# A hybrid delta-rule and mLSTM layer: gate rows in quarters on a ring of their own, scratch transfers later, and a first chunk made by hand

## The chip, the cores and the metric

The kernel runs on one core of one Trainium2 chip. The metric is the device time of one execution in microseconds (us), as the median of several runs. A core has five engines that take instructions in order, each from its own queue: TensorE (PE in the profile; matrix products and transposes), VectorE (DVE), ScalarE (ACT), GpSimd (POOL) and SyncE (SP), which here only issues DMA transfers. An instruction waits on semaphores for what it needs, and everything behind it on the same engine waits with it. On-chip memory is SBUF for operands and PSUM for results of products.

## The reference

One layer on x of 256 rows by 2048 columns, all float32. Of `reference.py`, cut to what matters here:

```python
shift, scale, gate = split(silu(c) @ w_ada + b_ada, 3)     # w_ada: 2048 x 6144
h = rms_norm(x, norm_pre_w) * (1 + scale) + shift
qkv, a, b, z, ml_qk, ml_v, ml_i, ml_f, ml_o, ml_z, g_A, g_B = split(h @ w_in)
# branch A: causal conv and silu on qkv, gated delta rule over 32 value heads in chunks of 64
#   (in each chunk a unit lower triangular system is solved), head norm, times silu(z)
y_A = o_a @ w_proj_gdn                                      # 4096 -> 2048
# branch B: conv and silu on ml_qk, chunkwise mLSTM over 8 heads, head norm, sigmoid(ml_o), silu(ml_z)
y_B = h_b @ w_proj_mlstm                                    # 2048 -> 2048
out = (sigmoid(g_A) * y_A + sigmoid(g_B) * y_B) @ w_out
return x + gate * rms_norm(out, norm_post_w)
```

## The kernel before, in words

Nearly all of the work is products of the 256 rows of h (later y and the merged rows) with weights that are read once. Each float32 operand is split into a high part that TensorE takes in one pass (`hi`, a cast on ACT, line 169) and the remainder (`lo`, a subtraction on VectorE or POOL, line 170), and each product is three: hi·hi, hi·lo, lo·hi (`mm3`, line 223).

**The stream.** `Stream` takes a list of units written out by hand. A weight unit is 1 MB: 128 partitions by 2048 columns, loaded by SP into `raw` of a ring of three buffers (`load_w`, line 164), prepared as two pieces of 1024 columns (`prep_w`: `whi`, `wlo`, four buffers each), and used piece by piece by TensorE. Preparation runs a few pieces ahead of use. A load is issued, in the order of the list, as soon as the unit that many places back on its ring has been prepared; a unit whose buffer isn't free holds every load behind it. During the start part POOL makes the remainder of some pieces in place of VectorE (`share`); the other pieces, and all later ones, are VectorE's.

**Side work.** After each used piece `side.step()` lets every open side generator run one step. All that isn't streaming, as the convolutions, decays, triangular inverses and norms, is written as generators whose `yield`s place their instructions between the pieces; `wait(n)` lets n steps pass, and `side.debt` and `side.room` hold back VectorE work where much of it stands in line. A piece takes TensorE about 2.7 to 3 us.

**The start.** `csil` is silu(c) spread over 128 partitions, made by eight products of one row (`one_row` by `crow`, line 282). For each chunk k of 128 of the 2048 columns of h, VectorE multiplies the two transposed rows of w_ada for shift and scale with `csil` and sums them (`ar` tiles, a ring of three of 1 MB, line 355). `x_scale` scales two chunks of x by the row norm on ACT (line 302), `x_turn` transposes them on TensorE and copies them back on ACT (lines 308 and 310). `h_chunk` makes shift and scale on ACT, then `hf` (ACT, line 333), `h_hi` (ACT), `h_lo` (VectorE or POOL). While these chunks come one by one, TensorE works on fourteen column groups of w_in that the branches don't need first (`START`, in seven `BLOCKS` of a range of k): partial sums over a few chunks are kept in `part` tiles (copies on ACT, line 413, additions on VectorE, line 411). The last two numbers of a block are the times, counted in w_ada rows, at which those rows are due in the list.

**The gdn periods.** Eight periods (`gdn_period`), each with three projections: q, k, v of a head pair, z, and q, k, v of the second pair. Behind the first and third follows `gdn_stage1`: convolution, decay rows `gb` read from DRAM (line 611), masks on POOL (line 618), exponentials on ACT (line 626), scores. `block_rows` writes the diagonal 32x32 blocks of the scores to DRAM (`ud`). `base_inverse` reads them back spread over partitions (`ug`), inverts them on VectorE, writes the result `xx` to DRAM (`xd`, line 745), reads it back in another order (`xcmp`, four transfers, line 748), copies it into `x0` on ACT (line 755) and transposes it into `ycmp` on VectorE (line 752). `gdn_stage2` uses both in small products (`mp`, line 781, to `po`). All of these transfers and the loads of the weights are issued by SP, in the order in which the steps reach them.

**mLSTM, gate and end.** Four mLSTM units follow. Among their weights stand sixteen units with the rows of w_ada for the gate (`add_gate_unit`), loaded on the ring of the weights; VectorE multiplies each by a value of `sil` and adds it to `gacc` in two halves of 1024 columns (line 1089). Then come the projections of y (`add_proj_y`, with `ya` read from DRAM and split into `yhi`, `ylo`), the merge and the output projection.

Of the kernel before, what the change touches and what calls it, by code (L numbers as in the profile page):

```python
# [117 lines left out]
def hybrid_layer_kernel(  # L118
# [51 lines left out]
        (eng or V).tensor_tensor(lo, src, hi.bitcast(F32), op=ALU.subtract)  # L170

    share = [-3072.0, START_SHARE]

    def split_w(src, hi, lo):

# [8 lines left out]
    def prep_w(h, raw, width=2048):  # L184
        n = min(1024, width - h * 1024)
        hi = wp.tile([P, 1024], F32R, name="whi", tag="whi", bufs=4)
        lo = wp.tile([P, 1024], F32R, name="wlo", tag="wlo", bufs=4)
        split_w(raw[:, h * 1024:h * 1024 + n], hi[:, 0:n], lo[:, 0:n])
        return hi, lo

# [35 lines left out]
    bp = x0 = y0 = None  # L226


    ct = const("ct", c_t, [P, KC])
    sil = cp.tile([P, KC], F32, name="sil")  # L230
    A.activation(sil, ct, AF.Silu)
# [36 lines left out]

    pcs = ExitStack()
    csil = pcs.enter_context(tc.tile_pool(name="pcs", bufs=1, space=PSUM)).tile([P, D], F32, name="csil")  # L270
    crow = [part[4 + i].rearrange("p b c -> p (b c)")[0:1] for i in range(2)]
    for i in range(2):
        SP.dma_start(crow[i], c_row[:, i * 1024:(i + 1) * 1024])
    for b in range(2):
        SP.dma_start(xs[:, b], x[b * P:(b + 1) * P])
    SP.dma_start(ident, consts[:, 0:128])
    bat = const("bat", b_ada_t, [P, 32])
    npre = const("npre", npre_t, [P, KC])
    for i in range(2):
        A.activation(crow[i], crow[i], AF.Silu)  # L280
    for q in range(4):
        T.matmul(csil[:, q * 512:(q + 1) * 512], one_row, crow[q // 2][:, (q % 2) * 512:(q % 2 + 1) * 512],
                 start=True, stop=True)
    late_c = {}

    def late_consts():
        SP.dma_start(con[:, 128:512], consts[:, 128:512])
        late_c.update(gcv=const("gcv", gconv, [P, 256]), mcv=const("mcv", mconv, [P, 64]),
                      abb=const("abb", ab_bias, [P, 1]), alog=const("alog", a_log, [32, 1]),
                      gnw=const("gnw", gnorm, [P, 1]), mnw=const("mnw", mnorm_t, [P, KC]))  # L290

    for b in range(2):
        A.activation(part[2].rearrange("p b c -> p (b c)"), xs[:, b, 0:1024], AF.Square, accum_out=ss[:, b, 0:1])
        V.scalar_tensor_tensor(part[3].rearrange("p b c -> p (b c)"), xs[:, b, 1024:D], 1.0, xs[:, b, 1024:D],
                               op0=ALU.mult, op1=ALU.mult, accum_out=ss[:, b, 1:2])
    V.tensor_reduce(rs, ss, axis=AX.X, op=ALU.add)
    V.tensor_scalar(rs, rs, 1.0 / D, EPS, op0=ALU.mult, op1=ALU.add)
    pow_(rs, rs, mhalf[:, 0:2])

    def x_scale(k):  # L300
        for b in range(2):
            A.activation(xs[:, b, k * P:(k + 2) * P], xs[:, b, k * P:(k + 2) * P], AF.Copy, scale=rs[:, b:b + 1])

    def x_turn(k):
        ps = jtile("xps")
        for b in range(2):
            for kk in range(2):
                T.transpose(ps[:, (b * 2 + kk) * P:(b * 2 + kk + 1) * P], xs[:, b, (k + kk) * P:(k + kk + 1) * P],
                            ident)
        A.copy(xs[:, :, k * P:(k + 2) * P], ps.rearrange("p (b c) -> p b c", b=2))  # L310
# [9 lines left out]
    V.scalar_tensor_tensor(bnp, bat[:, KC:2 * KC], 1.0, npre, op0=ALU.add, op1=ALU.mult)  # L320

    def load_ada(src):
        raw = sp.tile([P, 2048], F32, name="ar", tag="ar", bufs=ADA_BUFS)
        SP.dma_start(raw, src)
        return raw

    def h_chunk(k):

        A.activation(sh[:, k:k + 1], ad[:, k:k + 1], AF.Identity, bias=bat[:, k:k + 1])
        A.activation(s1[:, k:k + 1], ad[:, KC + k:KC + k + 1], AF.Identity, bias=bnp[:, k:k + 1],  # L330
                     scale=npre[:, k:k + 1])
        hf = sp.tile([P, S], F32, name="hf", tag="hf", bufs=2)
        A.activation(hf.rearrange("p (b t) -> p b t", b=2), xs[:, :, k * P:(k + 1) * P], AF.Identity, bias=sh[:, k:k + 1], scale=s1[:, k:k + 1])
# [6 lines left out]
    BLOCKS = ((EARLY, 0, 1, 1.1, 3.5), (REST, 0, 2, 4, 8), (EARLY, 1, 3, 8, 12), (REST, 2, 2, 12, 16.5),  # L340
              (ALL, 4, 4, 16.5, 26), (ALL, 8, 4, 26, 32), (ALL, 12, 4, 32, 32))
    due = []

# [5 lines left out]
    def ada_units():  # L349

        adders = []
        for k in range(KC):
            for pt in range(2):
                def prep(h, raw, k=k, pt=pt):
                    V.scalar_tensor_tensor(raw, raw, 1.0, csil, op0=ALU.mult, op1=ALU.mult,
                                           accum_out=ad[:, pt * KC + k:pt * KC + k + 1])
                    j = 2 * (2 * k + pt) - 4
                    if 4 <= j < 16:
                        x_turn(j)
                        if j < 12:  # L360
                            x_scale(j + 4)
                    h_chunks(k - 1)
                    if pt == 1:
                        due.append(k)
                        if k == 0:
                            h_chunks(0)
                        elif k == KC - 1:
# [27 lines left out]
    def add_start_groups(bi):  # L395
# [136 lines left out]
        stream.add(w_ab, prep_w, use, after=lambda: side.add(gates(st_["ps"])))  # L532

    ada = ada_units()
    ia = 0
    for bi, (groups, k0, nk, first, last) in enumerate(BLOCKS):
        if bi == len(BLOCKS) - 1:
            add_ab()
        fs = add_start_groups(bi)
        for j, f in enumerate(fs):  # L540
            ahead = first + (last - first) * j / len(fs)
            while ia < len(ada) and ia < ahead:
                ada[ia]()
                ia += 1
            f()

# [83 lines left out]
    def gdn_stage1(p, ps, res):  # L630
# [50 lines left out]
        for blk, ps_, n, c0 in ((0, psa, 256, 0), (1, psb, 128, 512)):  # L681
# [10 lines left out]
                pow_(sk, sse[:, 2:4], phalf[:, 0:2])  # L692
            else:
                scored[0] = p
        block_rows(res, z)
# [15 lines left out]

    def base_inverse(zg, res, zr):

        ud = res["ud"]
# [15 lines left out]
        for i in range(1, 32, 2):  # L730
# [10 lines left out]
            if w == 2:  # L741
                V.scalar_tensor_tensor(xx[:, 0:nq, i + 1], xx[:, 0:nq, i], nsu[:, i // 2:i // 2 + 1],
                                       xx[:, 0:nq, i + 1], op0=ALU.mult, op1=ALU.add)
        yield from wait(1)
        SP.dma_start(xd.rearrange("qq q rg m i -> (q rg m) qq i"), xx)
        xcmp = bp.tile([P, 8, 32], F32, name="xcmp", tag="xcmp", bufs=1)
        for q in range(4):
            SP.dma_start(xcmp[32 * q:32 * q + 32], xd[:, q])
# [3 lines left out]
        V.transpose(ycmp.rearrange("p m i -> p (m i)"), xcmp.rearrange("p m i -> p (m i)"))  # L752
# [317 lines left out]
    gate_at = [0, 0]  # L1070
    gate_half = []

    def add_gate_unit():

        gate_at[1] += KC
# [4 lines left out]
        gate_at[0] += 1  # L1080

        def prep(h, raw):
            side.debt += 2.4
            for q in range(2):
                if i == 0:
                    gate_half.append(bp.tile([P, 1024], F32, name=f"gacc{q}", tag=("ug", "rr")[q], bufs=1 + q))
                    V.tensor_scalar(gate_half[q], raw[:, q * 1024:(q + 1) * 1024], sil[:, 0:1], None, op0=ALU.mult)
                else:
                    V.scalar_tensor_tensor(gate_half[q], raw[:, q * 1024:(q + 1) * 1024], sil[:, i:i + 1],
                                           gate_half[q], op0=ALU.mult, op1=ALU.add)  # L1090
# [315 lines left out]
```

## Time and profile before

| | us |
|---|---|
| runs of the kernel before | 1602.19, 1605.75, 1607.46 (median 1605.75) |
| the profiled execution | 1603.88 |
| its span, first to last instruction | 1601.9 |
| TensorE busy | 1577.8 (98 %) |
| VectorE busy | 1150.1 (72 %) |
| ScalarE busy | 941.0 (59 %) |
| GpSimd busy | 236.7 (15 %) |

The span leaves out about 2 us of the execution. Times in rows are counted from the span's start. A timeline row gives the start, the duration, the engine, the line in the kernel, the operation, output and inputs with their shapes, how many such operations follow each other, and in brackets the idle time before them and what ended it; SPq is SP's queue of DMA issues. TensorE's matmuls overlap, so the duration of one is longer than the distance to the next. The mean granted clock of TensorE is 0.999.

### The profile page before, as it was taken

Reading aid. Unit: us, or ns where it says so; the run is one execution under the profiler, and the core shown is the slowest. Engines: PE = TensorE matmul, PEld = TensorE weight load, DVE = VectorE, ACT = ScalarE, POOL = GpSimd, SP = SyncE. Lnnn points to the kernel's source line nnn. Section 1 sums busy time; section 2 is a strip of 40 time slices with the busy share of each in tenths; the row PEclk is TensorE's granted clock in tenths of the full one; section 3 lists DMA queues with packets and bytes.
Section 4 is the critical chain, followed back from the end, with each engine's and each line's share of the span. In section 5 each row is a group of like instructions: output and inputs, shape, how many; then the busy total and the mean of one; then the engine's idle time right before and its main releaser. Section 6 shows DMA issues by size and latency. Waiting matters only on the chain.

```text
span 1601.9 us, 25461 instructions
## 1 busy us (share of the span) xinstructions
PE 1577.8 (98%) x9844; PEld 1388.1 (87%) x9844; DVE 1150.1 (72%) x1801; ACT 941.0 (59%) x1503; POOL 236.7 (15%) x193
## 2 busy tenths in 40 slices
PE   7999999999999999999999999999999999999998
PEld 4888888899999999999999999889988888888886
DVE  6695556765689788887888788776878556756654
ACT  7754446765656575757576666655565644444443
POOL 1787771000000010000000000000000000100100
PEclk9999999999999999999999999999999999999999
DMA  9898775965565646564656465566888667766573
GB/s 375 339 406 335 279 274 195 289 238 191 170 203 175 205 148 204 164 193 169 193 169 195 149 197 176 187 214 247 290 308 305 227 249 284 283 246 244 200 273 113
DMA packets 96261, 372.37 MB, mean 232 GB/s; under 512 B 26262, under 2 KB 46214, under 8 KB 58252
## 3 DMA queue, kind: packets, MB, share of 16 engines
q1 hardware_dynamic: 96140, 370.75, 66.2%
q8 instruction: 77, 1.26, 0.3%
q14 instruction: 44, 0.36, 0.1%
HBM read 354.40 MB, written 16.31 MB: 231 GB/s over the span
## 4 chain that ended last, share of the span: by engine, by line
PE 79%; issue 13%; DMA 3%; DVE 2%; ACT 2%; POOL 1%; SPq 0%; DVEq 0%; POOLq 0%; ACTq 0%
PE pn L223 35%; PE pt L223 28%; PE py L223 8%; DMA raw<-in_dram 1%; POOL mg L1196 1%; PE psa L223 1%; ACT whi L169 1%; DVE wlo L170 1%; DMA ya<-o_dr 1%; DMA ar<-in_dram 1%; PE mz L816 0%; PE mq L807 0%; PE pa L828 0%; PE po L856 0%; PE po L857 0%
## 5 line engine op out<-in xcount | busy, mean ns | idle before, releaser
L170 DVE TENSOR_TENSOR wlo<-raw,whi 128x1024 fp32r<-128x1024 f32 x454 | 561.5, 1245 | 253.9 <-ACT whi L169 248.8
L169 ACT CAST whi<-raw 128x1024 fp32r<-128x1024 f32 (+1 forms) x517 | 533.0, 1046 | 327.1 <-PE pn L223 148.1
L223 PE MATMUL pt<-h_hi,whi 128*128 128x256 f32 x1280 | 367.8, 287 | 0.0
L223 PE MATMUL pt<-h_hi,wlo 128*128 128x256 f32 x1280 | 362.0, 283 | 0.0
L223 PE MATMUL pt<-h_lo,whi 128*128 128x256 f32 x1280 | 362.0, 283 | 0.0
L223 PE MATMUL pn<-whi,h_hi 128*128 128x512 f32 x896 | 353.9, 395 | 6.6 <-ACT whi L169 5.7
L223 PE MATMUL pn<-wlo,h_hi 128*128 128x512 f32 x896 | 350.0, 391 | 1.1 <-POOL wlo L170 0.6
L223 PE MATMUL pn<-whi,h_lo 128*128 128x512 f32 x896 | 349.8, 390 | 0.0
L223 PEld LDWEIGHTS pt<-h_hi,whi 128*128 128x128 f32 x1280 | 245.3, 192 | 1.4
L223 PEld LDWEIGHTS pt<-h_lo,whi 128*128 128x128 f32 x1280 | 245.4, 192 | 0.3
L223 PEld LDWEIGHTS pt<-h_hi,wlo 128*128 128x128 f32 x1280 | 245.2, 192 | 0.0
L223 PEld LDWEIGHTS pn<-whi,h_hi 128*128 128x128 f32 x896 | 168.8, 188 | 42.5 <-ACT whi L169 6.1
L223 PEld LDWEIGHTS pn<-wlo,h_hi 128*128 128x128 f32 x896 | 168.8, 188 | 36.0 <-DVE wlo L170 1.3
L223 PEld LDWEIGHTS pn<-whi,h_lo 128*128 128x128 f32 x896 | 168.6, 188 | 35.3
L170 POOL TENSOR_TENSOR wlo<-raw,whi 128x1024 fp32r<-128x1024 f32 (+1 forms) x63 | 146.3, 2332 | 67.1 <-ACT whi L169 64.9
L223 PE MATMUL py<-whi,yhi 128*128 128x512 f32 x384 | 150.6, 392 | 0.7 <-ACT vt L1017 0.7
L223 PE MATMUL py<-whi,ylo 128*128 128x512 f32 x384 | 149.6, 390 | 0.0
L223 PE MATMUL py<-wlo,yhi 128*128 128x512 f32 x384 | 149.4, 389 | 0.0
L411 DVE TENSOR_TENSOR part<-pn,part 128x512 f32<-128x512 f32 x112 | 73.7, 685 | 52.6 <-PE pn L223 52.6
L169 ACT CAST yhi<-ya 128x512 fp32r<-128x512 f32 x48 | 29.9, 622 | 130.9 <-PE py L223 127.4
L170 DVE TENSOR_TENSOR ylo<-ya,yhi 128x512 fp32r<-128x512 f32 x48 | 33.2, 692 | 86.7 <-ACT yhi L169 78.7
L593 DVE SCALAR_TENSOR_TENSOR qs<-pt,gcv,qs 128x255 f32<-128x255 f32 (+2 forms) x192 | 92.2, 480 | 4.6
(251 smaller groups left out, 1790.8 us busy)
## 6 DMA issues: line engine op xcount, KB each, us to landing
raw<-in_dram SPq DMA_DIRECT2D x259, 1024.0 KB
ar<-in_dram SPq DMA_DIRECT2D x32, 1024.0 KB
raw<-in_dram SPq DMA_DIRECT2D x16, 512.0 KB
ya<-o_dr SPq DMA_DIRECT2D x32, 256.0 KB
gate_dr<-part SPq DMA_DIRECT2D x11, 512.0 KB
gb<-rows SPq DMA_DIRECT2D x20, 256.0 KB
raw<-in_dram SPq DMA_DIRECT2D x6, 768.0 KB
ug<-ud SPq DMA_DIRECT2D x32, 128.0 KB
```

What stands on the lines that cost most here:

```text
L169: A.copy(hi, src)
L170: (eng or V).tensor_tensor(lo, src, hi.bitcast(F32), op=ALU.subtract)
L223: T.matmul(ps, l, r, start=start and i == 0, stop=stop and i == 2, skip_group_check=True)
L411: V.tensor_tensor(part[g][:, b], ps[b], part[g][:, b], op=ALU.add)
L593: V.scalar_tensor_tensor(dst[:, n, sh:], src[:, 0:S - sh], taps(n, 3 - sh), dst[:, n, sh:], op0=ALU.mult, op1=ALU.add)
L1196: G.tensor_tensor(mcols(b, hf, cg), mcols(b, hf, cg), s_, op=ALU.add)
```

## The change

Four parts.

1. *The start.* `c_row` is issued from ACT's queue, `ar0` (the first shift row) ahead of x on SP, the first scale row `ar1` in two halves behind x; three small constants are issued from POOL's queue; `ct` and its silu move to the later constants. A function `first_chunk` takes the place of the preparation of the first weight piece: it puts five calls of a float32 product of zeros behind csil on TensorE, the squares of x's rows (three of four on ACT, one on VectorE), the norm's small steps on POOL, the two sums of chunk 0 on VectorE, the copy of the first `whi` on VectorE, x_scale(0), x_turn(0), another product of zeros, and makes `hf` straight from PSUM. x_turn(2), x_scale(4) and x_scale(6) move in between the first groups. The units of w_ada start at chunk 1; one pair of due times goes from 12 to 13.
2. *h_chunk.* `h_lo` of the last chunk is VectorE's.
3. *Scratch.* `block_rows` comes one step later; `base_inverse` begins with a step, and its wait for `ug` is one step shorter; `xd` is written one step later; `xcmp` is read two steps after that, and used two steps on in place of five.
4. *Gate rows.* Each unit is loaded as four quarters of 512 columns into buffers of `yhi` and `ylo`, on a ring "gate" of one, and summed in four quarters.

```diff
-    crow = [part[4 + i].rearrange("p b c -> p (b c)")[0:1] for i in range(2)]
-    for i in range(2):
-        SP.dma_start(crow[i], c_row[:, i * 1024:(i + 1) * 1024])
+    crow = ada_tile()[0:1]
+    A.dma_start(crow, c_row)
+    ar0, ar1 = load_ada(w_ada[0]), ada_tile()
     for b in range(2):
         SP.dma_start(xs[:, b], x[b * P:(b + 1) * P])
-    SP.dma_start(ident, consts[:, 0:128])
-    bat = const("bat", b_ada_t, [P, 32])
-    npre = const("npre", npre_t, [P, KC])
+    for t, src in ((bat, b_ada_t), (npre, npre_t), (ident, consts[:, 0:128])):
+        G.dma_start(t, src)
...
+    def keep_busy(n):
+
+        for _ in range(n):
+            T.matmul(zps, zero[:, 0:P], zero, start=True, stop=True)
...
-        A.copy(xs[:, :, k * P:(k + 2) * P], ps.rearrange("p (b c) -> p b c", b=2))
-    for k in range(0, 8, 2):
-        x_scale(k)
-        if k in (2, 4):
-            x_turn(k - 2)
+        if k:
+            A.copy(xs[:, :, k * P:(k + 2) * P], ps.rearrange("p (b c) -> p b c", b=2))
...
+    def first_chunk(src, hi, lo):
+        keep_busy(5)
...
+        ada_sum(ar0, slice(0, D), ad[:, 0:1])
+        V.scalar_tensor_tensor(bnp, bat[:, KC:2 * KC], 1.0, npre, op0=ALU.add, op1=ALU.mult)
+        for i in range(2):
+            ada_sum(ar1, half[i], adh[:, i:i + 1])
...
+        V.tensor_copy(hi, src)
+        x_scale(0)
+        xps = x_turn(0)
+        keep_busy(1)
+        V.tensor_tensor(lo, src, hi.bitcast(F32), op=ALU.subtract)
+        hf = sp.tile([P, S], F32, name="hf", tag="hf", bufs=2)
+        A.activation(hf.rearrange("p (b t) -> p b t", b=2), xps[:, :, 0], AF.Identity, bias=sh[:, 0:1],
+                     scale=s1[:, 0:1])
+        split(hf, h_hi[:, 0], h_lo[:, 0], V)
+        A.copy(xs[:, :, P:2 * P], xps[:, :, 1])
+        x_scale(2)
...
-        split(hf, h_hi[:, k], h_lo[:, k], V if k < 2 else G)
+        split(hf, h_hi[:, k], h_lo[:, k], V if k in (1, KC - 1) else G)
...
-    (EARLY, 1, 3, 8, 12), (REST, 2, 2, 12, 16.5),
+    (EARLY, 1, 3, 8, 13), (REST, 2, 2, 13, 16.5),
...
+                    if bi == 0 and gg == 3:
+                        x_turn(2)
+                    elif gg == (NE - 1, NE)[min(bi, 1)] and c == 0 and bi < 2:
+                        x_scale(4 + 2 * bi)
...
+        yield
         block_rows(res, z)
-        yield
...
     def base_inverse(zg, res, zr):
+        yield
...
-        yield from wait(4)
+        yield from wait(3)
...
-        yield from wait(1)
+        yield from wait(2)
         SP.dma_start(xd.rearrange("qq q rg m i -> (q rg m) qq i"), xx)
+        yield from wait(2)
...
-        yield from wait(5)
+        yield from wait(2)
...
+    def load_gate(src):
+        raw = [yp.tile([P, 512], F32, name=f"graw{q}", tag=("yhi", "ylo")[q % 2], bufs=2) for q in range(4)]
+        for q in range(4):
+            SP.dma_start(raw[q], src[:, q * 512:(q + 1) * 512])
+        return raw
...
-            side.debt += 2.4
-            for q in range(2):
+            side.debt += 2.6
+            for q in range(4):
...
-        stream.add(w_ada[32 + i], prep, None, 1)
+        stream.add(w_ada[32 + i], prep, None, 1, load=(load_gate, "gate", 1))
```

More of the change, by code (lines that the diff above doesn't have):

```diff
@@ L172, in hybrid_layer_kernel @@
     share = [-3072.0, START_SHARE]
+    begin = []
     def split_w(src, hi, lo):
@@ L187, in prep_w @@
         lo = wp.tile([P, 1024], F32R, name="wlo", tag="wlo", bufs=4)
+        if begin:
+            begin.pop()(raw[:, 0:n], hi, lo)
+            return hi, lo
         split_w(raw[:, h * 1024:h * 1024 + n], hi[:, 0:n], lo[:, 0:n])
@@ L270, in hybrid_layer_kernel, with ada_tile, load_ada, silu_c @@
     csil = pcs.enter_context(tc.tile_pool(name="pcs", bufs=1, space=PSUM)).tile([P, D], F32, name="csil")
-    crow = [part[4 + i].rearrange("p b c -> p (b c)")[0:1] for i in range(2)]
-    for i in range(2):
-        SP.dma_start(crow[i], c_row[:, i * 1024:(i + 1) * 1024])
+    def ada_tile():
+        return sp.tile([P, 2048], F32, name="ar", tag="ar", bufs=ADA_BUFS)
+    def load_ada(src):
+        raw = ada_tile()
+        SP.dma_start(raw, src)
+        return raw
+    crow = ada_tile()[0:1]
+    A.dma_start(crow, c_row)
+    ar0, ar1 = load_ada(w_ada[0]), ada_tile()
     for b in range(2):
         SP.dma_start(xs[:, b], x[b * P:(b + 1) * P])
-    SP.dma_start(ident, consts[:, 0:128])
-    bat = const("bat", b_ada_t, [P, 32])
-    npre = const("npre", npre_t, [P, KC])
+    bat = cp.tile([P, 32], F32, name="bat")
+    npre = cp.tile([P, KC], F32, name="npre")
+    for t, src in ((bat, b_ada_t), (npre, npre_t), (ident, consts[:, 0:128])):
+        G.dma_start(t, src)
     for i in range(2):
-        A.activation(crow[i], crow[i], AF.Silu)
+        SP.dma_start(ar1[:, i * 1024:(i + 1) * 1024], w_ada[1][:, i * 1024:(i + 1) * 1024])
+    for i in range(2):
+        A.activation(crow[:, i * 1024:(i + 1) * 1024], crow[:, i * 1024:(i + 1) * 1024], AF.Silu)
     for q in range(4):
-        T.matmul(csil[:, q * 512:(q + 1) * 512], one_row, crow[q // 2][:, (q % 2) * 512:(q % 2 + 1) * 512],
-                 start=True, stop=True)
+        T.matmul(csil[:, q * 512:(q + 1) * 512], one_row, crow[:, q * 512:(q + 1) * 512], start=True, stop=True)
+    zero = part[-1][:, 0]
+    G.memset(zero, 0.0)
+    zps = jtile("zps")
+    def keep_busy(n):
+        for _ in range(n):
+            T.matmul(zps, zero[:, 0:P], zero, start=True, stop=True)
     late_c = {}
+    def silu_c():
+        yield
+        yield
+        A.activation(sil, ct, AF.Silu)
     def late_consts():
         SP.dma_start(con[:, 128:512], consts[:, 128:512])
+        SP.dma_start(ct, c_t)
+        side.add(silu_c())
         late_c.update(gcv=const("gcv", gconv, [P, 256]), mcv=const("mcv", mconv, [P, 64]),
@@ new lines, in x_turn, with ada_sum @@
+        return ps.rearrange("p (b k t) -> p b k t", b=2, k=2)
+    bnp = sp.tile([P, KC], F32, name="bnp")
+    adh = sp.tile([P, 2], F32, name="adh")
+    def ada_sum(raw, cols, out):
+        V.scalar_tensor_tensor(raw[:, cols], raw[:, cols], 1.0, csil[:, cols], op0=ALU.mult, op1=ALU.mult,
+                               accum_out=out)
+    def first_chunk(src, hi, lo):
+        keep_busy(5)
+        half = [slice(i * 1024, (i + 1) * 1024) for i in range(2)]
+        for b in range(2):
+            for i in range(2):
+                if b == 0 and i == 1:
+                    V.scalar_tensor_tensor(part[3].rearrange("p b c -> p (b c)"), xs[:, b, half[i]], 1.0,
+                                           xs[:, b, half[i]], op0=ALU.mult, op1=ALU.mult, accum_out=ss[:, b, i:i + 1])
+                else:
+                    A.activation(part[2].rearrange("p b c -> p (b c)"), xs[:, b, half[i]], AF.Square,
+                                 accum_out=ss[:, b, i:i + 1])
+        G.tensor_tensor(rs, ss[:, :, 0], ss[:, :, 1], op=ALU.add)
+        G.tensor_scalar(rs, rs, 1.0 / D, EPS, op0=ALU.mult, op1=ALU.add)
+        pow_(rs, rs, mhalf[:, 0:2])
+        ada_sum(ar0, slice(0, D), ad[:, 0:1])
+        V.scalar_tensor_tensor(bnp, bat[:, KC:2 * KC], 1.0, npre, op0=ALU.add, op1=ALU.mult)
+        for i in range(2):
+            ada_sum(ar1, half[i], adh[:, i:i + 1])
+        V.tensor_tensor(ad[:, KC:KC + 1], adh[:, 0:1], adh[:, 1:2], op=ALU.add)
+        V.scalar_tensor_tensor(s1[:, 0:1], ad[:, KC:KC + 1], npre[:, 0:1], bnp[:, 0:1], op0=ALU.mult, op1=ALU.add)
+        A.activation(sh[:, 0:1], ad[:, 0:1], AF.Identity, bias=bat[:, 0:1])
+        V.tensor_copy(hi, src)
[9 more added lines that the diff above has]
+        x_scale(2)
@@ L327, in h_chunk @@
+    begin.append(first_chunk)
     def h_chunk(k):
@@ L351, in ada_units @@
         adders = []
-        for k in range(KC):
+        for k in range(1, KC):
             for pt in range(2):
@@ L541, in hybrid_layer_kernel @@
             ahead = first + (last - first) * j / len(fs)
-            while ia < len(ada) and ia < ahead:
-                ada[ia]()
+            while ia - 2 < len(ada) and ia < ahead:
+                ada[ia - 2]()
                 ia += 1
```

36 lines of the change are left out of this document (13 added, 23 removed).

## The prediction

> **What bounds the kernel now.** I read the page's busy shares first, then TensorE's waits grouped by releaser (columns: total us, count, longest), and then the timeline around each of them.
>
> ```profile
> span 1601.9 us, 25461 instructions
> PE 1577.8 (98%) x9844; PEld 1388.1 (87%) x9844; DVE 1150.1 (72%) x1801; ACT 941.0 (59%) x1503; POOL 236.7 (15%) x193
> PE pn L223 <- ACT whi L169: 5.7, 1, 5.7
> PE csil L282 <- ACT part L280: 3.9, 1, 3.9
> PE mp L781 <- DVE ycmp L752: 1.9, 1, 1.9
> PE xps L308 <- ACT xs L302: 1.3, 1, 1.3
> PE py L223 <- ACT vt L1017: 0.7, 1, 0.7
> PE pn L223 <- POOL wlo L170: 0.6, 1, 0.6
> PE pa L828 <- ACT x L817: 0.5, 1, 0.5
> PE pn L223 <- ACT part L413: 0.5, 1, 0.5
> PE pab L223 <- POOL h_lo L170: 0.4, 1, 0.4
> ```
>
> TensorE is busy for 98 % of the span. The waits shown come to 15.5 us, and 10.9 of these (5.7 + 3.9 + 1.3) lie ahead of the first product. The change removes hardly any TensorE work, so what can be won is these waits and the products run at half clock after the start; what can be lost is any new wait. All the waits after 100 us are single events: one at the end of the start part (pab), three late (mp, pa, py).
>
> ```profile
> 3.88 7.19 PE L282 MATMUL csil<-part,one_row 1*128 1x512 f32 x8 [3.88 <-ACT part L280]
> 12.37 1.97 PE L308 MATMUL xps<-con,xs 128*128 128x128 f32 x8 [1.30 <-ACT xs L302]
> 20.00 0.80 PE L223 MATMUL pn<-whi,h_hi 128*128 128x512 f32 x1 [5.67 <-ACT whi L169]
> 21.27 0.79 PE L223 MATMUL pn<-wlo,h_hi 128*128 128x512 f32 x1 [0.47 <-DVE wlo L170]
> 24.84 0.45 PE L223 MATMUL pn<-whi,h_hi 128*128 128x512 f32 x1
> 34.12 1.04 PE L308 MATMUL xps<-con,xs 128*128 128x128 f32 x8
> 9.26 1.06 ACT L293 ACTIVATE part<-xs 128x1024 f32<-128x1024 f32 x1 [1.43 <-DMA xs<-in_dram]
> 12.80 2.29 DVE L355 SCALAR_TENSOR_TENSOR ar<-ar,csil 128x2048 f32<-128x2048 f32 x1 [1.73 <-DMA ar<-in_dram]
> 17.97 0.60 ACT L333 ACTIVATE hf<-xs,sh,s 128x256 f32<-128x256 f32 x1
> 18.60 0.40 ACT L169 CAST h_hi<-hf 128x256 fp32r<-128x256 f32 x1
> ```
>
> The eight csil products take 0.90 us each, and the transposes after them are still slow: 1.97 us for eight against 1.04 at 34.12. The first products take 0.80, and 0.45 at 24.84. So full speed comes about 3.6 us after the products begin to run without a gap (24.84 − 21.27), and the 7.19 us of csil did not bring it.
>
> **Part 1, the last h_lo on VectorE.**
>
> ```profile
> 262.79 0.73 POOL L170 TENSOR_TENSOR h_lo<-hf,h_hi 128x256 fp32r<-128x256 f32 x1 [23.59 <-ACT h_hi L169]
> 32.10 0.42 DVE L170 TENSOR_TENSOR h_lo<-hf,h_hi 128x256 fp32r<-128x256 f32 x1 [0.20 <-ACT h_hi L169]
> ```
>
> 0.73 − 0.42 = **+0.3** of the pab wait; nothing if VectorE is in a piece of 1.2 us just then.
>
> **Part 2, the start.** The change loads the first shift row ahead of x and makes the first chunk by hand, with ten half products of zeros (five calls of two instructions, as each csil product is two) between csil and the first transpose. The loads: x's second half landed at 9.26, the first `ar` at 12.80. With `ar` first, x's second half comes one load later, 12.8 at most (the 3.54 between those rows holds three small issues as well); three issues fewer stand ahead of it on SP's queue, and I take 10.8 to 12.8. TensorE: csil ends at 3.88 + 7.19 = 11.1 as now. Ten zero products at 0.90 would end at 20.1; if full speed comes 3.6 us after 11.1, four run at 0.90 and six at 0.45, and they end near 17.4 (16.9 to 18.6). x_turn(0) stands behind them: about 0.9 at full speed, then hf 0.60 and h_hi 0.40, first product near 19.3 (18.9 to 20.6). The other inputs: VectorE's sums are 2.29 and the same again in two halves, some 2.6, from 11.1 to 16.0, and two small ones to 16.4; on ACT two squares of 1.06 after x's landing, three small ones on POOL of at most 0.73, and x_scale of 0.9 end at 16.0 to 18.1, the late end being inside the range just given. So the zeros most likely set the time, and the first product comes 0.7 us earlier than 20.00 and at full speed: the 3.6 us from 21.27 on take half, 1.8 less. Upper end of the gain 2.5.
>
> The Trainium skill ("TensorE: Matmul & The Clock Gate", Part 1 on the HAM clock gate) says that about one window of some 3.4 us of busy TensorE doubles the clock. The 3.6 us above agree; the 7.19 us of csil at 0.90 each do not, and they have a single row of contraction. By the page alone csil would have warmed the array already, the ten zeros would take 4.5 us and the gain would be about 1.5 us larger; no term below uses this.
>
> Who takes the gain is ACT:
>
> ```profile
> 14.06 0.91 ACT L302 ACTIVATE xs<-xs,rsx 128x256 f32<-128x256 f32 x2
> 14.87 0.57 ACT L310 COPY xs<-xps 128x512 f32<-128x512 f32 x1
> 18.91 1.99 ACT L169 CAST whi<-raw 128x1024 fp32r<-128x1024 f32 x2
> 48.78 1.08 ACT L413 COPY part<-pn 128x512 f32<-128x512 f32 x2
> 18.00:60.00 42.00, 38.23 (x68) 1.00 0.95 379
> 25.00:60.00 35.00, 33.25 (x61) 1.00 0.94 375
> ```
>
> (The last two are ACT's alone: window, length, busy.) From 25 to 60 us ACT is busy for 95 % and TensorE's wait near 49 is for ACT's copy. The change moves work from ahead of hf to behind it: x_scale of chunks 2, 4 and 6 (0.91 each), the copies of x_turn(2) (0.57) and of the second half of x_turn(0) (about 0.35), less one whi of 1.0 that VectorE now makes: 2.65 us by durations, some 2.3 without the overlapped latency. ACT has 42.00 − 35.00 − (38.23 − 33.25) = 2.0 us of idle before 25 to put it in. It therefore reaches the copy of 48.78 as late after hf as now, plus 0.3 to 0.6, and hf starts at 17.9 to 19.5 (now 17.97). TensorE then waits there longer by what it gained; moreover x_turn(2) runs in line on it for 0.9. Bounds: 1.5 us lost (hf at 19.5) to 2.5 won (ACT not binding). Nearest is ACT's row of 95 %, so near zero; since the small waits of 0.6 and 0.5 (pn from POOL and ACT) can shrink, I take **+0.3**. The other moved items (constants on POOL's queue, the silu of c to the late constants, POOL's pieces one later, the pair of due times) sit on queues idle there or under ACT's work: 0, at worst within these ends.
>
> **Part 3, scratch transfers later.** SP issues everything in order. The issues and their followers in period 2, which stands for periods 1 to 6:
>
> ```profile
> 654.89 2.76 SPq L748 DMA_DIRECT2D xcmp<-xd  x4
> 657.75 4.03 SPq L164 DMA_DIRECT2D raw<-in_dram  x2
> 661.87 0.38 SPq L611 DMA_DIRECT2D gb<-rows  x1
> 663.83 1.68 ACT L755 COPY x<-xcmp 32x256 f32<-32x256 f32 x4
> 667.16 0.82 POOL L618 TENSOR_SCALAR_AFFINE_SELECT dd<-gb 128x256 f32<-128x256 f32 x2 [9.08 <-DMA gb<-rows]
> 672.87 1.23 DVE L170 TENSOR_TENSOR wlo<-raw,whi 128x1024 fp32r<-128x1024 f32 x1 [2.26 <-ACT whi L169]
> 676.80 0.39 PE L223 MATMUL pn<-wlo,h_hi 128*128 128x512 f32 x1
> ```
>
> There is no TensorE wait in these periods, so nothing can be won. The step of L755's copies stays (1 + 5 = 2 + 2 + 2 steps), but xcmp is now issued behind the second raw (issued at 661.4) at 662.1 to 664.8. gb, issued there now, lands behind that raw just before POOL's 667.16; xcmp in its place lands near 666.9. The copies, in order on ACT, wait there until 666.9 instead of 663.83, 3.1 us; behind them stand the exponentials of the decay (whose gb is issued 2.8 later too, behind xcmp's four issues) and whi, then wlo: 672.87 + 1.23 + 3.1 = 677.2, needed at 676.80. A stall of 0.4, six times: **−2.2**. Bounds: 0 (xcmp lands before 666.5) and −10 (1.3 us later than I think, 1.7 each). ud, ug and xd one step later shift VectorE's inverse by up to a piece, inside the steps that its waits leave.
>
> **Part 4, the late waits and the gate's rows.** In the waits of the queues, then in the timeline:
>
> ```profile
> SPq L164 <- DVE gacc L1089: 34.1, 15, 4.2
> L1089 DVE SCALAR_TENSOR_TENSOR gacc<-raw,sil,gacc 128x1024 f32<-128x1024 f32 x30 | 37.2, 1282 | 1.4 <-DMA raw<-in_dram 1.4
> 1072.13 2.00 ACT L169 CAST whi<-raw 128x1024 fp32r<-128x1024 f32 x2 [4.41 <-DMA raw<-in_dram]
> 1235.49 0.62 ACT L169 CAST yhi<-ya 128x512 fp32r<-128x512 f32 x1 [1.54 <-DMA ya<-o_dr]
> ```
>
> In the last gdn period SP stands at xcmp until xd has landed while raws queue behind, ACT then waits 4.41 for a raw, and VectorE's ycmp is late: the mp wait, 1.9. With xd two steps ahead of xcmp SP does not stand there; +1.9. The waits of pa and py (0.5 and 0.7) follow raws and a ya (ACT's 1.54) held in SP's queue until a gate sum frees a raw buffer; on a ring of their own the rows hold none: +1.2. All 3.1; I take **+2.8**, as other transfers move into those places. Bounds: 3.1, and 0 if each wait only finds another transfer ahead of it. VectorE's 2 sums of 1.28 become 4 of about 0.7 (0.2 more per unit); it is 72 % busy overall, and no TensorE wait in that part is for it but ycmp: 0.
>
> **Sum:** 0.3 + 0.3 − 2.2 + 2.8 = 1.2 us won. The profiled run took 1603.88 (span 1601.9 and 2.0 around it), 1.87 under the median of 1605.75. From the one 1602.7, from the other 1604.5; I give **1603.3**.
>
> **Rivals.** *The zeros don't lift the clock* (so the start doesn't do what it says), as csil's seven us did not. Then they end near 20, the transposes take up to 1.97, hf starts near 21.5 instead of 17.97, and ACT carries 3.5 us on: −3.5 + 0.3 − 2.2 + 2.8 = 2.6 lost, 1606.5. For it: csil's row. Against: zeros have 128 rows as the products that did lift it. Chance 0.15. *All gains arrive:* ACT gives way (2.5 instead of 0.3), xcmp lands in time (0 instead of −2.2), late 3.1: 5.9 won, 1598.0. For it: the stall of 0.4 hangs on a landing I know to 1 us; against: ACT's 95 %. Chance 0.28. *Slower:* xcmp lands 1.3 us later than 666.9, as two raws can be ahead of it; ACT's copies hold whi, and TensorE stalls 1.7 in each of six periods, 10.2 lost against 3.4 won: 1610.7. It decides from a landing after 668. Chance 0.10. Forecast 0.43; 0.04 for others, shared by both sides.
>
> **How the numbers follow.** 0.3 % is 4.8 us, so faster means under 1600.9 and slower over 1610.6. Faster: 0.28 + 0.02 = 0.30; slower 0.10 + 0.02, of which about 0.02 stays inside, so 0.10; within: 0.43 + 0.15 and that rest, 0.60. Range 1597 to 1609: the second rival's time at one end, the clock rival's and most of the bounds of part 3 at the other.
>
> **What would show it.** Right: zero products of 0.9 that become 0.45 near 14.7; a first product at 18.9 to 20.6 of 0.4 to 0.5; a PE wait on ACT near 49 longer than now; L755's copies waiting for the DMA of xcmp in periods 1 to 6 with short PE waits behind; no mp, pa and py waits. Wrong: zero products at 0.9 throughout; no wait on ACT before 60; more than 1 us of PE wait in any middle period, or no wait of ACT for xcmp.

## The result and the profile after

| | us |
|---|---|
| before, median beside it | 1606.58 |
| after, median | 1616.38 (1613.53 to 1620.77) |
| ratio of after to before | 1.0066, 95 % interval 1.0048 to 1.0084 |
| profiled execution of after | 1620.77, span 1619.0 |

The change makes the kernel slower by about 10 us. The forecast was 1603.3 with a range up to 1609; the measured median lies above both. The page of the kernel after, and TensorE's waits in it (us in total, times, longest):

```profile
span 1619.0 us, 25615 instructions
PE 1592.3 (98%) x9856; PEld 1391.2 (86%) x9856; DVE 1153.3 (71%) x1835; ACT 938.6 (58%) x1503; POOL 239.3 (15%) x198
PE pn L227 <- DVE wlo L170: 4.9, 7, 1.1
PE csil L297 <- ACT ar L295: 3.7, 1, 3.7
PE pnum L1029 <- issue: 2.0, 1, 2.0
PE pn L227 <- POOL wlo L170: 1.9, 1, 1.9
PE pc L904 <- DVE rr L897: 1.3, 3, 1.0
PE psa L227 <- DVE ql L699: 1.3, 3, 0.5
PE py L227 <- ACT whi L169: 0.9, 1, 0.9
PE pn L227 <- ACT part L465: 0.8, 1, 0.8
PE py L227 <- DVE wlo L170: 0.8, 1, 0.8
PE py L227 <- ACT vt L1075: 0.7, 1, 0.7
```

The wait of 5.7 us for the first `whi`, the one of 1.3 for `x_scale`, and those of mp, pa and pab are gone, as the change intends. In their place stand waits for VectorE (wlo, rr, ql: 7.5 us in thirteen pieces) and a group late (pnum, py). A stall shifts the products behind it by more than the wait shown (near 760 us 0.77 is shown and 1.14 shifted), so the shifts below come to more than the waits.

To see where the time went, each product of one trace was set against the same product of the other (the k-th of its group with the k-th), and the difference of their starts read off at a few places. Positive is later than before, in us; the columns are times in the trace of before:

```
kernel                      30     57    275   1060   1083   1190   1260
after                    -2.18  +0.43  -0.53 +12.58 +10.45  +9.70 +16.78
start+gate (e1)          -2.44  +0.22  -0.77  -0.74  -2.87  -3.62  +1.97
e1, xd/xcmp later (e2)   -2.31  +0.36  -0.63  +2.52  +0.39  -0.36  +3.77
start+scratch (e3)       -2.14  +0.47  -0.49 +11.19  +9.06  +8.31  +9.78
start only (e4)          -1.99  +0.61  -0.35  -0.35  +1.21  +0.44  +1.49
after, wait(4) (e5)      -2.02  +0.62  -0.34  +5.73  +3.60  +3.72  +9.38
e4, POOL later (e6)      -1.87  -0.69  -1.63  -1.62  -0.26  -0.77  -0.42
e4, no zeros (e7)        -2.28  -1.08  -2.06  -1.29  -0.31  -0.37  +0.23
e1, looser gate (e8)     -2.27  -1.09  -2.04  -2.04  -4.17  -4.92  -5.95
e4, zeros of 1 row (e9)  +2.86  +4.05  +3.10  +3.12  +3.98  +4.39  +5.01
best (e10)               -1.84  -0.65  -1.62  -0.93  -3.05  -3.81  -4.75
e8, xd/xcmp later (e11)  -1.74  +0.84  -0.12  +2.29  +0.17  -0.59  -1.55
e8, ud/ug later (e12)    -1.43  +1.13  +0.16  +2.11  -0.01  -0.77  -1.80
```

After 1260 nothing changes any more. The row of after reads: 2.2 us won at the start and lost again by 57; 0.96 won by 275 (0.35 of it at 263, the h_lo, the rest a wait near 85 that is gone); **13.1 lost between 275 and 1060**; 2.1 and 0.75 won at the old mp and pa waits; **7.1 lost between 1190 and 1260**.

Each row compares one execution with one other. The trace of after is its longest (1620.77, 4.4 us over its median) and the trace of before lies 2.7 us under its median, so the 16.8 us of the last column are 7 more than the 9.8 between the medians. The middle's loss is typical: start+scratch, whose trace lies 0.4 us over its median, has 11.7 there. The late loss of after is not: 3.4 us of it come from a stretch at half clock, as shown below.

**The start.** TensorE after:

```profile
10.82 6.54 PE L305 MATMUL zps<-part 128*128 128x512 f32 x10
18.94 0.50 PE L227 MATMUL pn<-whi,h_hi 128*128 128x512 f32 x1 [0.28 <-ACT h_hi L169]
38.61 0.70 PE L227 MATMUL pn<-wlo,h_hi 128*128 128x512 f32 x1 [1.88 <-POOL wlo L170]
39.11 0.63 PE L227 MATMUL pn<-whi,h_lo 128*128 128x512 f32 x1
42.36 0.40 PE L227 MATMUL pn<-wlo,h_hi 128*128 128x512 f32 x1
38.70:42.10 3.40, 3.40 (x9) 0.51 1.04 420
```

The zeros end at 17.4 and the first product comes at 18.94 at nearly full speed, as forecast (17.4 and 19.3). Then, at 38.61, TensorE waits 1.88 us for POOL's first remainder, and the products behind it run at half speed for about 3 us (0.63 long, 0.43 apart in place of the later 0.23), some 1.5 us more. The last row is a stretch of PE alone (window, length, busy, products, granted clock, share and GB/s of DMA): the granted clock is 0.51.

**The middle.** VectorE's waits for `ug`, before and after, and one period's transfers and first use of ug, before and after:

```profile
DVE nsu L725 <- DMA ug<-ud: 2.0, 2, 1.2
679.59 1.75 SPq L709 DMA_DIRECT2D ud<-au  x4
684.73 3.04 SPq L718 DMA_DIRECT2D ug<-ud  x4
699.06 0.14 DVE L725 TENSOR_SCALAR nsu<-ug 128x15 f32<-128x15 f32 x1
```

```profile
DVE nsu L782 <- DMA ug<-ud: 24.7, 7, 5.6
DVE nsu L782 <- issue: 3.8, 1, 3.8
681.92 1.75 SPq L765 DMA_DIRECT2D ud<-au  x4
690.73 0.35 SPq L164 DMA_DIRECT2D raw<-in_dram  x1
691.13 2.97 SPq L775 DMA_DIRECT2D ug<-ud  x4
704.47 0.17 DVE L782 TENSOR_SCALAR nsu<-ug 128x15 f32<-128x15 f32 x1 [5.55 <-DMA ug<-ud]
ACT x L813 <- DMA xcmp<-xd: 17.2, 11, 2.5
```

VectorE stands 28.5 us in all before the inverse, where it stood 2.0. In the period shown ug is issued 6.4 us later, behind one more weight load, and used by the program at the same step. TensorE's stalls begin at 722 us, behind this wait.

**The end.** SP's waits for the gate's sums, before and after, then the issues and ACT's wait that lead to the stall near 1248, and TensorE's clock behind it:

```profile
SPq L164 <- DVE gacc L1089: 34.1, 15, 4.2
```

```profile
SPq L1135 <- DVE gacc L1157: 70.8, 46, 10.8
1235.57 3.24 SPq L1135 DMA_DIRECT2D graw<-in_dram  x4
1239.34 0.43 SPq L1200 DMA_DIRECT2D ya<-o_dr  x1
1246.66 0.62 ACT L169 CAST yhi<-ya 128x512 fp32r<-128x512 f32 x1 [5.48 <-DMA ya<-o_dr]
1250.40:1257.20 6.80, 6.12 (x15) 0.51 0.94 334
```

SP now stands 70.8 us at the gate's quarters, twice as long as it stood at a raw buffer held by a gate unit. The quarters issued at 1235.57 have weight loads and `ya` behind them; ACT waits 5.48 us for a ya and TensorE for ACT. (The wait of pnum, near 1201, is another gap of this part; e3 and e8 are without it.) Behind the stall TensorE runs 6.8 us at a granted clock of about a half, which costs 3.4 of the 7.1 us lost. The same stall brought half as long a stretch in e1 (0.51 from 1236.9 to 1240.3, 1.7 us) and none in e2; without the clock's share the loss from 1190 to 1260 is 3.7 to 4.1 us in all three.

### The profile page after: what moved, and what is told of

Its sections match the earlier page's. It is cut to its first block, busy times and chain, and to the rows that moved or that the text cites. A ratio compares the mean times of both kernels' runs of the same rounds, so it can differ in the third digit from the quotient of the medians.

```text
span 1619.0 us, 25615 instructions
## 1 busy us (share of the span) xinstructions
PE 1592.3 (98%) x9856; PEld 1391.2 (86%) x9856; DVE 1153.3 (71%) x1835; ACT 938.6 (58%) x1503; POOL 239.3 (15%) x198
## 4 chain that ended last, share of the span: by engine, by line
PE 61%; issue 14%; DVE 12%; DMA 6%; ACT 3%; POOL 2%; SPq 1%; DVEq 0%; ACTq 0%; POOLq 0%
PE pn L227 29%; PE pt L227 18%; PE py L227 8%; DVE wlo L170 5%; DMA ug<-ud 2%; DVE qs L649 1%; DVE tmp L793 1%; DVE au L741 1%; DVE xx L797 1%; DMA xd<-xx 1%; DMA gb<-rows 1%; POOL mg L1263 1%; DVE xx L799 1%; DMA ya<-o_dr 1%; ACT whi L169 1%
## 5 line engine op out<-in xcount | busy, mean ns | idle before, releaser
L169 ACT CAST whi<-raw 128x1024 fp32r<-128x1024 f32 x516 | 530.8, 1047 | 308.4 <-PE pn L227 138.2
```

Source lines behind the costliest of these rows:

```text
L169: A.copy(hi, src)
```

## The experiments

All edits are to the kernel after unless said otherwise. Each time is the median, with the ratio to runs of the kernel before on the same chip and its 95 % interval.

### e1: scratch as before

```diff
-        yield
         block_rows(res, z)
+        yield
...
     def base_inverse(zg, res, zr):
-        yield
...
-        yield from wait(3)
+        yield from wait(4)
...
-        yield from wait(2)
+        yield from wait(1)
         SP.dma_start(xd.rearrange("qq q rg m i -> (q rg m) qq i"), xx)
-        yield from wait(2)
...
-        yield from wait(2)
+        yield from wait(5)
```

> The changed kernel with part 3 (all four scratch transfers) as before; start, h_lo and gate as changed. Theory U (the scratch delays cost the middle of the kernel: VectorE's waits for ug there come to 28 us in the changed kernel, 2 in the one before): VectorE's waits for ug fall to 2 us, TensorE loses nothing between 270 and 1040 us, the mp wait of about 2 us is back, and the late waits of the gate's rows stay, so about 1610 to 1613. Rival (the middle is late because of the start or of the lower mean clock of 0.996): 1615 to 1617, and TensorE waits between 700 and 1040 us stay.

1604.34 us, ratio 0.9989 (0.9979 to 1.0000), well under both expectations. The middle loses nothing (-0.77 to -0.74), so part 3 is the whole of the 13 us; by the two ratios (1.0066 and 0.9989) part 3 costs 12.4 us. Contrary to the expectation the mp wait did not come back (-0.74 to -2.87): the gate part alone removes it, as the scratch part alone does in e3. The late losses stay (5.6 us between 1190 and 1260, 1.7 of it half clock).

### e2: only ud and ug as before

The first three edits of e1.

> The changed kernel with only ud and ug as before (issued a step earlier, the wait one step longer); xd and xcmp stay later. Theory U (VectorE stands at ug, which now is issued behind a weight load and used one step sooner): the middle loses 0 to 2 us in place of 13, ACT's waits for xcmp of 2.3 to 2.5 us each stay; about 1606 to 1610. Rival X (the prediction's own: xcmp behind a weight load holds ACT's copies and whi behind them): the middle still loses 10 or more, 1614 to 1617.

1609.56 us, 1.0023 (1.0012 to 1.0034). The middle loses 3.15 us in place of 13.1, somewhat over Theory U's 0 to 2. So the loss is mostly gone without the moves of ud and ug, but xd and xcmp are not free.

### e3: gate rows as before

The new `load_gate` and its ring taken out, the two sums of 1024 columns restored.

> The changed kernel with the gate rows as before (whole units on the ring of the weights). Theory S (a ring of one for the gate makes SP stand at each quarter until VectorE has summed the one before, with weights and ya behind it): the TensorE gaps near 1201 (2.1 us) and 1247 to 1252 (4.5 us) of the changed kernel go, 1609 to 1612, with the loss of the middle left. Rival (these gaps come from the middle's backlog or from the scratch order): 1615 to 1617.

1613.29 us, 1.0045 (1.0030 to 1.0060), between the two expectations; the interval overlaps that of after (1.0048 to 1.0084). The middle's loss stays (11.7); of the late losses the 1201 gap is gone, and between 1190 and 1260 1.5 us are lost in place of 7.1.

### e4: the start and the h_lo alone

e1 and e3 together.

> Only the new start and the h_lo of the last chunk; scratch and gate as before. Theory: by the two traces TensorE is 0.5 us ahead of the kernel before from 264 us on, so 1605 to 1607, with the waits of mp, pa and py as before. Rival (the start leaves VectorE or POOL behind for the rest): over 1609.

1605.56 us, 0.9998 (0.9988 to 1.0009): no difference.

### e5: one step more before the inverse

```diff
-        yield from wait(3)
+        yield from wait(4)
         yield from side.room(0.8)
```

> The changed kernel, but base_inverse waits four steps instead of three between the issue of ug and VectorE's first use of it (the inverse then begins one step later than before the change). Theory W (what costs is that VectorE, in order, arrives at ug before its packets, 3.5 to 5.6 us in six periods): these waits fall below 3 us each and the total to under 12 of 28 us; the time falls from 1616 to about 1608 to 1611, near that of the kernel with only xd and xcmp later (1609.6). Rival (the transfers' place in the queue, or the later end of the inverse, costs): 1614 to 1618.

1612.80 us, 1.0047 (1.0031 to 1.0062), above what Theory W said and under the rival's range; the interval overlaps that of after. VectorE and TensorE in this kernel:

```profile
DVE nsu L782 <- DMA ug<-ud: 7.6, 4, 3.2
PE psa L227 <- DVE ql L699: 2.7, 6, 0.5
```

The waits for ug fall from 28.5 to 7.6 us and the middle's loss in the traces from 13.1 to 6.1. What is left is mostly six waits of TensorE for `ql`, one in each period, of at most 0.5 us, which shift it by 4.4 us in all; after has three of them. That the later inverse pushes `ql` back on VectorE is argued from the order of its instructions, and e5 keeps the later xcmp as well, which cost 3.15 in e2.

### e6, e7: what takes the start's gain

To e4, POOL's first remainder one piece later (e6), and no products of zeros (e7):

```diff
-    share = [-3072.0, START_SHARE]
+    share = [-3891.2, START_SHARE]
```

```diff
-        keep_busy(5)
...
-        keep_busy(1)
```

> Only the new start (scratch and gate as before), with POOL's first remainder one piece later again (the share begins at -3891 in place of -3072). Theory P (the start's lead of 3 us at 25 us is lost where POOL's 2.4 us remainder stands behind a late whi: TensorE waits 2.05 us near 37 and then runs 3 us at half clock, 1.6 us more): the wait falls under 1 us, no half clock follows, TensorE is 1.5 to 3 us ahead at 55 us, 1602.5 to 1604.5. Rival A (the recorded one: ACT is the bound, so the wait only moves to another piece): at 60 us within 0.7 us of the kernel before, 1605 to 1606.5.

> Only the new start, without any product of zeros (the computation is unchanged by it). Theory: the first transposes wait only for x_scale (about 15.7) and run at half speed, the first product comes at about 17.7 at half clock, full speed 3.6 us after it; the lead at 25 us is 1 to 2 us in place of 3, and since the lead is lost by 50 us anyway the kernel takes 1604.5 to 1606.5. Rival (the zeros carry the start): first product no earlier, 2 us or more lost, over 1607.

e6 took 1604.02 us, 0.9992 (0.9984 to 1.0001); e7 1604.89, 1.0004 (0.9992 to 1.0015): neither can be told from before. TensorE's waits in e6, then the first products of e7:

```profile
PE pn L227 <- ACT part L465: 1.8, 3, 1.0
PE pn L227 <- DVE wlo L170: 0.7, 1, 0.7
```

```profile
15.40 1.12 PE L331 MATMUL xps<-con,xs 128*128 128x128 f32 x4 [3.96 <-ACT xs L324]
17.77 0.80 PE L227 MATMUL pn<-whi,h_hi 128*128 128x512 f32 x1 [1.25 <-ACT h_hi L169]
21.50 0.39 PE L227 MATMUL pn<-whi,h_lo 128*128 128x512 f32 x1
```

In e6 POOL's wait is gone and no half speed follows, but three waits for ACT's copies and one for a remainder stand there instead: at 57 us 0.7 us are won, not 1.5 to 3. The position is the rival's and the time Theory P's, so the two aren't separated; the waits name ACT, as the forecast did, but no run gives ACT less work. In e7 the first product comes 1.2 us earlier than in after, at half speed until 21.5, and TensorE is as far at 30 us (-2.28 against -1.99): the zeros buy nothing. e7 has the same wait of 1.9 us near 38 but no half speed after it, so it keeps 1.7 us more at 275 than e4. Its zeros are not the reason: e8 has them, has the same wait and no half speed either, and is at -2.04. That the clock falls back after such a wait is not sure each time: it did in after, e1 to e5, e11 and e12, and not in e7, e8 and e9.

### e8: weights may pass a gate unit

To e1, in `Stream`: a gate unit whose buffers are not free is passed over, and its buffers count as free one piece later.

```diff
-        while self.loaded < len(self.units):
-            u = self.units[self.loaded]
+        for u in self.units[self.loaded:]:
+            if "raw" in u:
+                continue
             if u["before"] is not None and not u["before"]["done"]:
-                return
+                if u["ring"] == "gate":
+                    continue
+                break
...
-                u["done"] = last
+                for v in self.after_prep:
+                    v["done"] = True
+                self.after_prep = [u] if last and u["ring"] == "gate" else []
+                u["done"] = last and u["ring"] != "gate"
```

> Start and gate as changed, scratch as before; but weight loads may be issued ahead of a gate unit whose buffers are not yet free, and a gate unit's buffers count as free one piece later. Theory S (in the changed kernel SP stands at the gate's quarters until VectorE has summed the unit before, with weights and ya behind): the TensorE gaps near 1188 (1.8 us) and 1233 to 1240 (3.8 us) of start plus gate go, 1598 to 1601. Rival (the quarters' transfers themselves are what delays weights and ya): the gaps stay, 1603 to 1606.

1599.85 us, 0.9966 (0.9954 to 0.9979), faster than both kernels. All of TensorE's waits of 0.3 us or more that the view shows, and SP's at the gate:

```profile
PE csil L305 <- ACT ar L303: 3.7, 1, 3.7
PE pn L235 <- POOL wlo L178: 1.9, 1, 1.9
PE pn L235 <- ACT part L473: 1.3, 1, 1.3
PE pn L235 <- ACT h_hi L177: 0.3, 1, 0.3
SPq L1141 <- DVE gacc L1163: 21.1, 43, 2.5
```

No such wait after 300 us is left. SP's standing at the gate falls from 69.3 us in e1 (70.8 in after) to 21.1, and the late losses of e1 (5.6, or 3.9 without its half clock) become a gain of 1.0. Between e1 and e8 the ratios differ by 3.7 us. The quarters as such cost nothing; the order in which they were asked for did.

### e11, e12: the two halves of the scratch part, each alone

On e8, xd and xcmp later as in the change (e11); ud and ug later as in the change (e12).

> Start, gate with the loosened loads, and of the scratch part only xd and xcmp later. Theory X (the prediction's own price of 2.2 us for the middle: ACT waits 2.3 to 2.5 us for xcmp and whi behind it is late): ACT waits for xcmp in six or seven periods, the middle from 270 to 1060 us loses 2 to 4 us, no more is lost late: 1602 to 1604 against 1599.85. Rival (this part costs 5 us by itself, as it did beside the strict gate ring): over 1604.5.

> Start, gate with the loosened loads, and of the scratch part only ud and ug later with the wait of three steps. Theory U: VectorE waits for ug 20 us or more in all, TensorE loses 5 to 10 us between 500 and 1060 us, waiting for VectorE's products: 1605 to 1610. Rival (ug costs only together with xcmp): 1600 to 1602.

e11 took 1602.55 us, 0.9988 (0.9979 to 0.9997); e12 1601.01, 0.9977 (0.9968 to 0.9986). The middle loses 2.4 us in e11, as theory X said, and 1.95 in e12, whose time is in the rival's range and not in theory U's (by the ratios, 3.5 and 1.8 us against e8); together they lose 13.1 in after. The same period as above, first e11 with its waits for xcmp and TensorE's waits from 275 to 1062 us, then e12:

```profile
682.04 1.75 SPq L773 DMA_DIRECT2D ud<-au  x4
687.17 3.01 SPq L782 DMA_DIRECT2D ug<-ud  x4
700.73 0.17 DVE L789 TENSOR_SCALAR nsu<-ug 128x15 f32<-128x15 f32 x1 [1.66 <-DMA ug<-ud]
ACT x L820 <- DMA xcmp<-xd: 15.8, 7, 2.5
PE pn L235 <- DVE wlo L178: 0.9, 2, 0.6
```

```profile
680.00 1.75 SPq L773 DMA_DIRECT2D ud<-au  x4
689.29 2.87 SPq L783 DMA_DIRECT2D ug<-ud  x4
700.42 0.17 DVE L790 TENSOR_SCALAR nsu<-ug 128x15 f32<-128x15 f32 x1 [1.13 <-DMA ug<-ud]
```

This fits why the sum is more than its two parts. From the last issue of ug to its landing passed 700.73 − 690.18 = 10.6 us and 700.42 − 692.16 = 8.3 us (in after 704.47 − 694.10 = 10.4). Before, 699.06 − 687.77 = 11.3 us were there, so the room was 1 to 3 us. The later xcmp brings ud 2.45 us later (679.59 to 682.04), about what ACT waits for xcmp in each period (2.5), and ug with it; the moved step alone brings ug 4.6 later; both 6.4. Each alone uses the room up and waits a little; together VectorE waits 5.55. In e11 ACT waits 2.4 to 2.5 us for xcmp in six periods, from 585 to 993 us, but TensorE stalls only behind the sixth, at 1007 and 1014: the five before it cost it nothing. How a wait of ACT for xcmp reaches ud (through the exponentials and the scores behind it) is argued from the order of the instructions, not shown by a run.

### e10 and e9: the best of it, and zeros of one row

e10 is e8 with the edits of e6 and e7. e9 is e4 with the products of zeros contracting one row:

```diff
-            T.matmul(zps, zero[:, 0:P], zero, start=True, stop=True)
+            T.matmul(zps, zero[0:1, 0:P], zero[0:1], start=True, stop=True)
```

> Start without zeros, POOL's first remainder one piece later, gate with the loosened loads, scratch as before. Theory (ACT caps the start's gain at 1.6 to 2 us whether or not POOL's wait or the zeros are there; the late waits are gone by the gate part): 1598.5 to 1600.5, the same as with zeros and POOL's wait. Rival (the start's gains add up): under 1598.

> Only the new start, with the zero products contracting one row in place of 128 (as csil does). Theory (products of one row don't bring TensorE to full speed, as the 7 us of csil don't): all ten take 0.85, end near 19.5, the transposes and the first products run at half speed, first product after 21. Rival (any stream of products does, and csil is only too short by phase): 0.43 from about 15 us as with 128 rows.

e10 took 1598.97 us, 0.9961 (0.9948 to 0.9975), not to be told from e8: the start's gains do not add up (-1.62 us at 275, as in e6, against -2.04 and -2.06 in e8 and e7). e9 took 1609.31 us in one run:

```profile
10.67 8.74 PE L305 MATMUL zps<-part 1*128 1x512 f32 x10
22.38 0.80 PE L227 MATMUL pn<-whi,h_hi 128*128 128x512 f32 x1
28.42 0.39 PE L227 MATMUL pn<-whi,h_lo 128*128 128x512 f32 x1
```

All ten stay at 0.87 us, where those of 128 rows fell to 0.43 (after about 4 us in after, 3.0 in e8, 5.8 in e12), and full speed comes only about 6 us after the first weight product.

## Why the prediction was wrong, by its own steps

- **Start: +0.3 forecast, about 0 measured** (e4). Right in size, and right in part in its mechanism: the zeros lift the clock, the first product comes as computed, and the gain is lost again. It is not lost where the forecast said: the wait for ACT near 49, which was to grow, was 0.45 before and is gone in after. The loss comes at 38.6, because ACT's late `whi` holds POOL, whose 2.4 us remainder turns it into one wait of 1.9 us, and because the clock can fall back behind that wait. Where it does not fall back the same start is 2.0 us ahead at 275 (e8), so the size is partly luck.
- **h_lo: +0.3 forecast, 0.35 measured.** Right.
- **xd and xcmp: −2.2 forecast for the middle, 2.4 measured alone** (e11). ACT's wait was put at 3.1 us and is 2.4, so by the prediction's own sum wlo ends at 672.87 + 1.23 + 2.4 = 676.5, before the 676.80 at which it is needed; ACT's copies start at 666.30 (forecast landing: 666.9), and the prediction's own bound for a landing before 666.5 was 0. Accordingly five of the six periods cost nothing, and the 2.4 us are lost behind the sixth, where VectorE also makes the mLSTM's convolution. The size is right by luck; the stall of 0.4 in each of six periods is not there.
- **The step that failed is the sentence that ud, ug and xd one step later shift the inverse "inside the steps that its waits leave", at 0.** It priced the moves by themselves and looked at VectorE's step, not at ug's issue on SP: moved a step it goes behind one more weight load and 4.6 us later, while its own wait was cut by a step. The room before, 11.3 us from the last issue at 687.77 to the use at 699.06, could have been read; the flight of 8 to 10 us was seen only in the later runs. And this delay adds to the one from xcmp, which the prediction had priced: 2.4 and 1.95 alone, 13.1 together. By the ratios the whole of part 3 cost 12.4 us (after against e1) where 2.2 were forecast, and the other parts together won 1.8 (e1, 0 to 3.4) where 3.4 were: part 3 is nearly all of the miss.
- **Late: +2.8 forecast, 4.2 lost in the trace of after** (2.1 and 0.75 won, 7.1 lost, of which 3.4 are half clock behind the stall). The three old waits did go, or nearly: mp 2.1, pa 0.75; py stayed. The failed half-sentence is that rows on a ring of their own "hold none": the loads are issued in the order of the list, so a ring of one holds every weight behind it until VectorE has done the sum before. e8 shows it: with weights free to pass, the late part wins 3.9 us from 1060 on. The mp wait was put down to SP standing at xcmp; e1 shows that the gate part removes it too. In the medians this step is small: between e4 and e1 the gate part wins 1.4 us, between e3 and after it loses 3.4, each with overlapping intervals.
- **The rivals.** That the time could go up by a delay growing past its slack in each period was there, with 0.10 and 1610.7, but at xcmp's landing, not at ug's. "All gains arrive" is almost e8: 1599.85 against 1598.0, reached by leaving the scratch part out and letting weights pass the gate. The rivals' times are counted from the profiled 1603.88, the forecast from a point between that and the median; from the median beside after the same sum gives 1605.4.

## What to carry to other kernels

When a transfer moves by a step, write down its issue, its landing and its first use, and count what SP now issues ahead of it; the room is a number in the trace, and two small delays of one chain must be added before each is called hidden. A ring of its own does not free the loads behind it while one queue issues all loads in the order of a list: a ring of one made SP stand 70.8 us here in place of 34.1. And before a trace is used to price a change, see how far its execution lies from the median.

## What the hardware showed that was not expected

- Products that contract one row do not bring TensorE to full speed: eighteen of them, 16 us nearly without a gap (3.68 to 19.4 in e9), stay at 0.87 to 0.90 us each; zeros of 128 rows reach 0.43 after 3.0 (e8) to 5.8 us (e12). Zeros count as work.
- A wait of TensorE of 1.9 us can be enough for half speed over the next 3.4 us. The Trainium skill ("TensorE: Matmul & The Clock Gate", Part 1) puts the idle time that does this at one window of about 3.4 us; here it took 1.9, though not every time (e7, e8 and e9 had the same wait without it). The mp wait of 1.90 us near 1080 is as uneven: before goes on at a granted clock of 1.00, e4 at 0.53 from 1080.6 to 1084.2.
- Which of the two happens fits the phase of a count of 3.41 us. In these traces each half-speed stretch amid the work begins a whole number of 3.41 us after full speed began (14.85 and 38.75 in after, 23.9 or 7 times 3.41 apart) and lasts 3.41 or twice that. Counted so, the wait near 38 lies whole within one such stretch in the eight traces that fall back, and is split by a boundary in the three that do not (in e8, where full speed began at 13.78, at 37.67, amid a wait from 36.65 to 38.52). The mp waits of before, e4, e6 and e7 agree; e9's, split and yet followed by half speed, does not. No run shifts the phase alone, so this is a reading of the traces, not a test.
